# Fewer, longer runs of small products among the large products of a gated DeltaNet decoder layer

## The chip, the cores and the metric

The kernel runs on one core of one Trainium2 chip. The metric is the time of one execution on the device in microseconds (us); lower is better. Three executions of the kernel before took 2884.91, 2886.78 and 2886.98 us, so the median is 2886.78 us.

The core has five engines that run beside one another, each with its own queue. PE multiplies matrices (the profile shows its weight loads apart, as PEld), DVE and ACT do elementwise work and read the products out of PSUM, POOL does some elementwise work in SBUF, and SP issues most of the DMAs. PSUM, into which PE writes, has eight banks; one product of 128 x 512 numbers in fp32 fills a bank.

## What is computed

The reference is one layer of a hybrid decoder with 512 tokens and width 2048. One projection, `h @ w_in`, feeds a branch of sliding-window attention and a branch of gated DeltaNet; the two are merged by gates and projected back. The change touches only the DeltaNet branch:

```python
d_qkv = causal_conv_silu(d_qkv, conv_w)
dq, dk, dv = jnp.split(d_qkv, [DN_KEY, 2 * DN_KEY], axis=-1)
...
t_inv = lax.linalg.triangular_solve(eye + L, ...)
u = t_inv @ v_beta
w = t_inv @ (k_beta * jnp.exp(g)[..., None])
qk = jnp.where(tril, jnp.einsum('bhncd,bhnsd->bhncs', q, k) * decay, 0.0)
...
def step(S, xs):
    u_c, w_c, qk_c, qd_c, kd_c, gl_c = xs
    v_new = u_c - w_c @ S
    o = qd_c @ S + qk_c @ v_new
    S = S * gl_c[..., None, None] + jnp.swapaxes(kd_c, -1, -2) @ v_new
    return S, o
```

There are 16 key heads of width 128 and 32 value heads, two to each key head. The state `S` goes through the sequence; the kernel takes it in four blocks of 128 tokens.

## The kernel before

**Large products.** Every projection is done as large products: weights and activations are split into a high and a low part (ACT casts the high part `whi` on L52, DVE subtracts for `wlo` on L53), and `mm3` (L251) issues three products of 128 x 512 for each block of 128 input channels: L254, L255 and L256. `channel_tile` (L258) makes one tile of 128 output channels by 512 tokens from 16 such blocks, 48 large products into one PSUM bank.

**Small work in steps.** After every second block, thus after every six large products, `channel_tile` calls `pump` (L81). One call of `pump` is called a *step* here. The small work is written as Python generators kept in the list `live`; `yield n` means "go on n steps later" (`step`, L124). So the order of the small work among the large products is fixed when the program is written, in the order of this list within a step. On the chip each engine takes its queue in order and starts each instruction as soon as its inputs are there; work that has its inputs early can run ahead of its step. Beside `live` there are slow generators (`solve`, for the inverse `t_inv` of the second half of the heads, on DVE, in groups 0 to 7) and side generators (`gate`, L1626, from group 8 on: multiply-adds on DVE, L1645, and at its end four products `pgate`, L1653, each of which holds a PSUM buffer until DVE has read it on L1655).

**A head group.** `heads` (L868) runs 16 times, once for a key head and its two value heads. A group makes five channel tiles, q, v0, v1, z0, z1, each with eight steps, so 40 steps; they are numbered 0 to 39 from the group's first. A tile's generator starts on the first step after its tile. What it puts on PE, by the step of its own group (from 40 on, the work lies in the next group's tiles, 40 steps less):

| step | work on PE | function and lines |
|---|---|---|
| 14 | `ptq`: 4 transposes of q | `queries`, L912 and L288 |
| 22 | `ptv` of v0: 4 transposes | `values`, L896 and L288 |
| 23 | `pqk`: query-key product, 8 instructions | `queries`, L951 to L953 |
| 25 | `py`: first product of the joined inverse, 16 instructions of 64 x 64 | L957 to L961 |
| 27 | `pu`: second product of it, 16 instructions of 64 x 64 | L965 to L968 |
| 30 | `ptv` of v1: 4 transposes | `values` |
| 33 | `pv` of block 0 | `scan`, L1000 |
| 35 | `pd` and `po` of block 0 | L1014 to L1021 |
| 37, 39, 41 | block 1: `pp`, `pv`, `pd` and `po` | L992, L1002, L1017 to L1021 |
| 43, 45, 47 | block 2: the same | |
| 49, 51, 53 | block 3: `pp`, `pv`, `po` | |
| 58, 59 | `pto`: 4 transposes of each of the two heads' results | L1056 to L1060 |

An fp32 product of full size is two instructions on PE, a transpose one. Behind `pqk` DVE multiplies it with the masks (tile `E` in the profile, L955); behind `py` DVE copies `Y` (L963); behind `pu` it makes the factors `tt` (L970); between `pp` and `pv` it makes `r` (L995), and between `pv` and `pd` ACT copies `vn` (L1004) and DVE scales `vs` (L1009). After the last block, DVE works out a row scale (L1045 to L1048, some ten short instructions) on step 55 and scales the results `osb` with it on step 56 (L1052). Behind each `pto` DVE multiplies with the gate tile `zh` (L1059); `head_sums` (L1064) sends sums of the two heads to memory from step 70 on. A group's chain thus runs on into the next group's tiles, and small work of two groups is interleaved.

**PSUM.** In this stage the eight banks are: two for the large products (pool `pmm`), two for `ptq`, `ptv`, `pqk`, `py`, `pu`, `pto` and `pgate` (pool `ptp`, tag `tp`), and four for `pp`, `pv`, `po`, `pd` (pool `psc`, tag `sc`). A product waits until the buffer that it is given is free.

After the sixteen groups come two more channel tiles of another kind (`merge_gate`, 16 steps). `drain_live` (L136) then issues what is left of the generators with no large products between, and the next stage, `branch_b`, opens its own PSUM pools over the same banks: six for large products, two for transposes.

Of the kernel before, what the change touches and what calls it, by code (L numbers as in the profile page):

```python
# [7 lines left out]
F32 = mybir.dt.float32  # L8
# [3 lines left out]
ALU = mybir.AluOpType  # L12
# [4 lines left out]
P = 128  # L17
T = 512
D = 2048
KT = D // P  # L20
NTB = T // P
# [4 lines left out]
HD = 64  # L26
# [3 lines left out]
TWO_PI_LO = 3.0199159819567e-07  # L30
MAGIC = float(0x5F3759DF)
NST = 4
NFIRST = 3
STW = 320 + NST * P


class Layer:
# [29 lines left out]

    def go(self, gen, delay=1):

        self.live.append([gen, delay])  # L70

    def paced(self, gen, budget):

# [7 lines left out]
    def pump(self):  # L81
        self.weight_tick()
        with self.behind() if self.keep_order else nullcontext():
            for e in list(self.live):
                e[1] -= 1
                if e[1] <= 0:
                    self.step(e)
        held, self.hold = self.hold > 0, max(self.hold - 1, 0)
        with self.behind():
            for e in [] if held else list(self.slow):  # L90
                e[2] += e[1]
                while e in self.slow and e[2] >= e[3]:
# [22 lines left out]
    def in_turn(self, op):  # L115
# [5 lines left out]
            )  # L121
        self.turn = op.ins.name

    def step(self, e):  # L124
        try:
            e[1] = next(e[0]) or 1
        except StopIteration:
            self.live.remove(e)

# [6 lines left out]
    def drain_live(self):  # L136
        while self.live:
            for e in list(self.live):
                e[1] -= 1
                if e[1] <= 0:  # L140
                    self.step(e)

    def drain_slow(self, e):
# [141 lines left out]
    def transpose4(self, dst, src_cols):  # L285

        for c in range(4):
            self.nc.tensor.transpose(dst[:, c * P : (c + 1) * P], src_cols(c), self.ident)  # L288


    def build(self):
# [599 lines left out]
    def values(self, wk, g, e, ps, st):  # L891
        nc = self.nc
        y = wk.tile([P, T], F32, tag="y", name="yv", bufs=3)
        yield from self.conv(wk, ps, 32 + 2 * g + e, y)
        yield 2
        pt = self.ptp.tile([P, T], F32, tag="tp", name="ptv")  # L896
        self.transpose4(pt, lambda c: y[:, c * P : (c + 1) * P])
        vt = wk.tile([P, NTB, P], F32, tag="vt", name="vt", bufs=3)
        nc.scalar.copy(out=vt.rearrange("p c d -> p (c d)"), in_=pt)
        st[f"v{e}"] = vt  # L900

    def queries(self, wk, g, ps, st):

        nc = self.nc
        sl = lambda c: slice(c * P, (c + 1) * P)
        q = wk.tile([P, T], F32, tag="y", name="yq", bufs=3)
        yield from self.conv(wk, ps, g, q)
        M = [self.decay_load(wk, 2 * g + e) for e in range(2)]
        kT = wk.tile([P, T], F32, tag="kT", name="kT")
        nc.sync.dma_start(out=kT, in_=self.kT_d[g])  # L910
        yield 2
        pt = self.ptp.tile([P, T], F32, tag="tp", name="ptq")  # L912
        self.transpose4(pt, lambda c: q[:, sl(c)])
        ss = self.sumsq(wk, pt)
        yield 3
        epsq = wk.tile([P, NTB], F32, tag="epsq", name="epsq")
        nc.vector.tensor_scalar(out=epsq, in0=ss, scalar1=EPS, scalar2=EPS * P, op0=ALU.add, op1=ALU.mult)
        yield 1
        for e in range(2):
            self.decay_mask(M[e], 2 * g + e)  # L920
        ta = wk.tile([P, NTB, HD], F32, tag="ta", name="ta", bufs=1)
        lab = wk.tile([P, NTB, HD], F32, tag="lab", name="lab", bufs=1)
        ts1 = wk.tile([P, NTB, HD], F32, tag="ts1", name="ts1", bufs=1)
        qd, TT = [], []
        for e in range(2):
            h = 2 * g + e
            qe = wk.tile([P, NTB, P], F32, tag="qe", name="qe", bufs=2)
            nc.sync.dma_start(out=qe.rearrange("p c i -> p (c i)"), in_=self.eg_rows[h].partition_broadcast(P))
            qd.append(qe)
            b, hl = h // 16, h % 16  # L930
            t = self.tt[h % 4]
            for k2 in range(2):
                s = slice(k2 * HD, (k2 + 1) * HD)
                nc.sync.dma_start(out=t[s, :, s], in_=self.ts_d[b, k2, hl].rearrange("c j i -> j c i"))
            s = slice(e * HD, (e + 1) * HD)
            nc.sync.dma_start(out=ta[s], in_=self.ta_d[b, hl].rearrange("c i j -> i c j"))
            nc.sync.dma_start(out=lab[s], in_=self.lab_d[h])
            if e:
# [12 lines left out]
        pqk = self.ptp.tile([P, NTB, P], F32, tag="tp", name="pqk")  # L951
        for c in range(NTB):
            nc.tensor.matmul(pqk[:, c, :], lhsT=kT[:, sl(c)], rhs=q[:, sl(c)], start=True, stop=True)  # L953
        for e in range(2):
            nc.vector.tensor_tensor(out=M[e], in0=pqk, in1=M[e], op=ALU.mult)  # L955
        yield 2
        py = self.ptp.tile([P, NTB, HD], F32, tag="tp", name="py")  # L957
        own = [slice(0, HD), slice(HD, P)]
        for c in range(NTB):
            for e in range(2):  # L960
                nc.tensor.matmul(py[own[1 - e], c, :], lhsT=lab[own[e], c, :], rhs=ta[own[e], c, :], start=True, stop=True)  # L961
        Y = wk.tile([P, NTB, HD], F32, tag="Y", name="Y", bufs=1)
        nc.vector.tensor_copy(out=Y, in_=py)  # L963
        yield 2
        pu = [self.ptp.tile([P, NTB, HD], F32, tag="tp", name="pu") for _ in range(2)]  # L965
        for c in range(NTB):
            nc.tensor.matmul(pu[0][0:HD, c, :], lhsT=Y[HD:P, c, :], rhs=TT[0][HD:P, c, HD:P], start=True, stop=True)
# [12 lines left out]
        yield from self.scan(wk, g, k, kT, TT, qd, M, epsq, st)  # L980

    def scan(self, wk, g, k, kT, TT, qd, M, epsq, st):
        nc = self.nc
        sl = lambda c: slice(c * P, (c + 1) * P)
        v = [st["v0"], st["v1"]]
        osb = wk.tile([P, 2, NTB, P], F32, tag="osb", name="osb", bufs=1)
        osq = wk.tile([P, 2, NTB], F32, tag="osq", name="osq")
        S = None
        for c in range(NTB):
            if c:  # L990
# [3 lines left out]
                for e in range(2):  # L994
                    nc.vector.scalar_tensor_tensor(  # L995
                        out=r[:, e, :], in0=pp[:, e, :], scalar=self.neg_eg[:, c, 2 * g + e : 2 * g + e + 1],
                        in1=v[e][:, c, :], op0=ALU.mult, op1=ALU.add,
# [5 lines left out]
            vn = wk.tile([P, 2, P], F32, tag="vn", name="vn", bufs=2)  # L1003
# [10 lines left out]
            po = self.psc.tile([P, 2, P], F32, tag="sc", name="po")  # L1014
# [3 lines left out]
            for e in range(2):  # L1018
                if c:
                    nc.tensor.matmul(po[:, e, :], lhsT=qd[e][:, c, :], rhs=S[:, e, :], start=True, stop=False)  # L1020
                nc.tensor.matmul(po[:, e, :], lhsT=M[e][:, c, :], rhs=vn[:, e, :], start=c == 0, stop=True)  # L1021
# [28 lines left out]
        for e in range(2):  # L1050
# [1 line left out]
            nc.vector.tensor_tensor(  # L1052
                out=of, in0=of, in1=ro[:, e * NTB : (e + 1) * NTB].unsqueeze(2).to_broadcast([P, NTB, P]), op=ALU.mult
            )
        yield 2
        for e in range(2):  # L1056
            pt = self.ptp.tile([P, T], F32, tag="tp", name="pto")
            self.transpose4(pt, lambda c: osb[:, e, c, :])
            nc.vector.tensor_tensor(out=z[e], in0=pt, in1=z[e], op=ALU.mult)  # L1059
            yield 1  # L1060
        yield 10
        yield from self.head_sums(wk, g, z)

    def head_sums(self, wk, g, z):  # L1064
# [674 lines left out]
```

## Time and profile before

| | us |
|---|---|
| median of three executions | 2886.78 |
| the profiled execution, its own time | 2883.98 |
| span of its records | 2882.2 |
| mean granted PE clock, share of full | 0.997 |
| PE busy | 2831.3 |
| DVE busy | 1869.0 |
| ACT busy | 1138.6 |

The span reaches from the first to the last recorded instruction; 1.8 us of the execution's own time lie outside it. The profile counts an engine as busy while one of its instructions is under way. Products on PE overlap in its pipeline, so the time that a product adds is the distance from its start to the next one's start and not its duration. The DeltaNet groups fill the stretch from about 540 to 1640 us of the span.

### The profile page before, as it was taken

The numbers are of one execution on the slowest core, as the hardware profiler recorded it, in microseconds if no ns is written. First come the engines' busy times: TensorE is split into PE (matmuls) and PEld (weight loads), VectorE is DVE, ScalarE is ACT, GpSimd is POOL, SyncE is SP. The second block draws the span as 40 slices with busy tenths as digits, with TensorE's granted clock in tenths as the row PEclk, the third lists the DMA queues.
The fourth block names the chain that finished last, engine by engine and source line by source line (L and its number), as shares of the span: only waits on it lengthen the run. The fifth ranks groups of instructions, "written<-read, shape, count | busy, mean of one in ns | idle before, by whom it ended". The sixth has DMA issues, their size and how long they took to land.

```text
span 2882.2 us, 38250 instructions
## 1 busy us (share of the span) xinstructions
PE 2831.3 (98%) x14428; PEld 2320.8 (81%) x14428; DVE 1869.0 (65%) x3020; ACT 1138.6 (40%) x2161; POOL 277.2 (10%) x266
## 2 busy tenths in 40 slices
PE   8899999999999999999999999999999999999999
PEld 6677888888888888888877888888887888788787
DVE  6765899777776556666665456665555655554565
ACT  4355333433334333433333355443343434432343
POOL 0013121101111111112110000000100100000000
PEclk9999999999999999999999999999999999999999
DMA  9756555636667867878863377675745647365575
GB/s 379 291 170 198 180 170 157 210 116 208 214 189 206 244 198 245 258 235 243 258 199 103 127 253 263 245 251 195 225 148 163 174 141 223 114 227 185 187 235 164
DMA packets 205471, 590.07 MB, mean 205 GB/s; under 512 B 74564, under 2 KB 99652, under 8 KB 154088
## 3 DMA queue, kind: packets, MB, share of 16 engines
q1 hardware_dynamic: 195080, 529.44, 53.8%
q0 software_dynamic: 10208, 58.20, 10.2%
q8 instruction: 113, 1.85, 0.3%
q14 instruction: 70, 0.57, 0.1%
HBM read 523.79 MB, written 166.40 MB: 239 GB/s over the span
## 4 chain that ended last, share of the span: by engine, by line
PE 85%; DVE 2%; issue 2%; DMA 2%; ACT 1%; POOL 0%; SPq 0%; DVEq 0%; POOLq 0%; ACTq 0%
PE mm L254 20%; PE mm L256 20%; PE mm L255 20%; PE od L254 3%; PE od L255 3%; PE od L256 3%; PE m L255 2%; PE m L256 2%; PE m L254 2%; PE S L1377 1%; PE pv L1002 1%; PE po L1021 1%; PE O L1428 1%; PE pP L288 1%; PE po L1020 1%
## 5 line engine op out<-in xcount | busy, mean ns | idle before, releaser
L254 PE MATMUL mm<-hh,whi 128*128 128x512 f32 x2784 | 1132.6, 407 | 2.3 <-ACT whi L52 1.6
L256 PE MATMUL mm<-hh,wlo 128*128 128x512 f32 x2784 | 1089.6, 391 | 1.0 <-DVE wlo L53 1.0
L255 PE MATMUL mm<-hl,whi 128*128 128x512 f32 x2784 | 1087.4, 391 | 0.0
L53 DVE TENSOR_TENSOR wlo<-raw,whi 128x1024 fp32r<-128x1024 f32 (+1 forms) x476 | 589.1, 1240 | 407.3 <-ACT whi L52 400.1
L52 ACT CAST whi<-raw 128x1024 fp32r<-128x1024 f32 (+1 forms) x476 | 495.3, 1044 | 813.0 <-PE mm L255 692.2
L256 PEld LDWEIGHTS mm<-hh,wlo 128*128 128x128 f32 x2784 | 522.6, 188 | 115.0 <-DVE wlo L53 1.9
L254 PEld LDWEIGHTS mm<-hh,whi 128*128 128x128 f32 x2784 | 523.7, 188 | 113.0 <-issue 9.6
L255 PEld LDWEIGHTS mm<-hl,whi 128*128 128x128 f32 x2784 | 524.2, 188 | 99.3 <-issue 1.4
L255 PE MATMUL od<-wlo,oh 128*128 128x512 f32 x448 | 174.6, 390 | 1.0 <-DVE wlo L53 1.0
L254 PE MATMUL od<-whi,oh 128*128 128x512 f32 x448 | 174.9, 391 | 0.0
L256 PE MATMUL od<-whi,ol 128*128 128x512 f32 x448 | 174.4, 389 | 0.0
L792 POOL TENSOR_TENSOR E<-E,neg_g 128x512 f32<-128x512 f32 x64 | 90.1, 1408 | 492.3 <-DMA E<-g_rows 354.8
L949 POOL TENSOR_TENSOR qe<-qe,yq 128x512 f32<-128x512 f32 x32 | 47.7, 1510 | 853.1 <-DMA qe<-eg_rows 676.4
L844 DVE TENSOR_TENSOR A<-A,atmp 128x62 f32<-128x62 f32 (+30 forms) x124 | 113.4, 914 | 1.5
L837 DVE TENSOR_TENSOR atmp<-A 128x62 f32<-128x62 f32 (+30 forms) x124 | 110.2, 889 | 1.4
L255 PEld LDWEIGHTS od<-wlo,oh 128*128 128x128 f32 x448 | 84.1, 188 | 18.6 <-DVE wlo L53 1.3
L256 PEld LDWEIGHTS od<-whi,ol 128*128 128x128 f32 x448 | 84.1, 188 | 17.6
L254 PEld LDWEIGHTS od<-whi,oh 128*128 128x128 f32 x448 | 84.1, 188 | 17.3 <-ACT whi L52 0.3
L53 DVE TENSOR_TENSOR wlo<-raww,whi 128x1024 fp32r<-128x1024 f32 x56 | 68.4, 1223 | 44.2 <-ACT whi L52 44.2
L52 ACT CAST whi<-raww 128x1024 fp32r<-128x1024 f32 x56 | 58.8, 1054 | 79.3 <-PE m L256 71.8
L995 DVE SCALAR_TENSOR_TENSOR r<-pp,neg_eg,vt 128x128 f32<-128x128 f32 x96 | 29.2, 346 | 73.5 <-PE pp L992 72.3
L1401 ACT ACTIVATE sm<-sm,mx,rs 128x256 f32<-128x256 f32 (+1 forms) x128 | 71.7, 562 | 3.3 <-DVE mx L1396 3.3
(341 smaller groups left out, 3267.1 us busy)
## 6 DMA issues: line engine op xcount, KB each, us to landing
raw<-in_w_ch SPq DMA_DIRECT2D x158, 1024.0 KB
wa<-in_w_ada_ss SPq DMA_DIRECT2D x32, 1024.0 KB
od_m<-in_w_od POOLq DMA_DIRECT2D x32, 1024.0 KB, 13.1
raw<-od_m SPq DMA_DIRECT2D x32, 1024.0 KB
raw<-in_w_od SPq DMA_DIRECT2D x24, 1024.0 KB
E<-g_rows SPq DMA_DIRECT2D x64, 256.0 KB
od_m<-in_w_od SPq DMA_DIRECT2D x16, 1024.0 KB
od_m<-od_m SPq DMA_DIRECT2D x16, 1024.0 KB
```

The costliest lines, as they stand in the source:

```text
L52: self.nc.scalar.copy(out=hi, in_=src)
L53: self.nc.vector.tensor_tensor(out=lo, in0=src, in1=hi.bitcast(F32), op=ALU.subtract)
L254: nc.tensor.matmul(ps, lhsT=wh, rhs=xh, start=first, stop=False)
L255: nc.tensor.matmul(ps, lhsT=wh, rhs=xl, start=False, stop=False)
L256: self.last_mm = nc.tensor.matmul(ps, lhsT=wl, rhs=xh, start=False, stop=last).ins
L288: self.nc.tensor.transpose(dst[:, c * P : (c + 1) * P], src_cols(c), self.ident)
L792: self.in_turn(nc.gpsimd.tensor_tensor(out=E, in0=E, in1=ng, op=ALU.add))
L837: eng.tensor_tensor(out=t, in0=A[:, m : m + 1, m + 1 :].to_broadcast([P, m, n]), in1=A[:, :m, m : m + 1].to_broadcast([P, m, n]), op=ALU.mult,
L844: eng.tensor_tensor(out=A[:, :m, m + 1 :], in0=A[:, :m, m + 1 :], in1=t, op=ALU.add)
L949: self.in_turn(nc.gpsimd.tensor_tensor(out=qf, in0=qf, in1=q, op=ALU.mult))
L995: nc.vector.scalar_tensor_tensor(out=r[:, e, :], in0=pp[:, e, :], scalar=self.neg_eg[:, c, 2 * g + e : 2 * g + e + 1], in1=v[e][:, c, :], ...
L1401: nc.scalar.activation(t, t, AF.Exp, scale=r[:, h : h + 1], bias=mx[:, h : h + 1], accum_out=den[:, h : h + 1])
```

## The change

Four kinds of small work (`ptq`, `ptv` of v0, `pu` and `pto`) are moved so that several come directly behind one another on PE. For this a generator may yield `JOIN + n`: from the next step on it is *late* for up to n + 1 steps, and goes on in the first of these in which another generator has already issued small products (their last instruction's name is left in `self.small`), or in the last of them in any case. Its PE instructions are then made to follow that last small product in PE's order, by an ordering edge without a semaphore (`step_joined`). Late generators are taken after all others of the step, in the list's order.

```diff
     def pump(self):
         self.weight_tick()
         with self.behind() if self.keep_order else nullcontext():
+            self.small = None
+            late = [e for e in self.live if e[2]]
             for e in list(self.live):
-                e[1] -= 1
-                if e[1] <= 0:
-                    self.step(e)
+                if e not in late:
+                    e[1] -= 1
+                    if e[1] <= 0:
+                        self.step(e)
+            for e in late:
+                e[2] -= 1
+                if self.small or not e[2]:
+                    self.step_joined(e)
...
+    def step_joined(self, e):
+
+        n, first = len(self.nc.cur_bb.bb.instructions), self.small
+        self.step(e)
+        for i in self.nc.cur_bb.bb.instructions[n:] if first else []:
+            if i.engine == mybir.EngineType.PE:
+                self.tc.add_manual_dep(
+                    i, first, mybir.DependencyInfo(mybir.DependencyClass.NoSync, mybir.DependencyReason.DATA), reason="join"
+                )
+
     def step(self, e):
+        e[2] = 0
         try:
             e[1] = next(e[0]) or 1
+            if e[1] >= JOIN:
+                e[1], e[2] = 1, e[1] - JOIN + 1
...
@@ values
         yield from self.conv(wk, ps, 32 + 2 * g + e, y)
-        yield 2
+        yield 1
+        yield 1 if e else JOIN + 1
@@ queries, ahead of ptq
-        yield 2
+        yield 1
+        yield JOIN + 1
...
@@ queries, ahead of pu
-        yield 2
-        pu = [self.ptp.tile([P, NTB, HD], F32, tag="tp", name="pu") for _ in range(2)]
+        yield 1
+        yield JOIN + 3
+        pu = [pool.tile([P, NTB, HD], F32, tag=tag, name="pu") for pool, tag in ((self.ptp, "tp"), (self.psc, "sc"))]
...
@@ scan, behind the scaling of osb
-        yield 2
+        yield 3
+        yield JOIN + 2
+        pts = [self.psc.tile([P, T], F32, tag="sc", name="pto") for _ in range(2)]
         for e in range(2):
-            pt = self.ptp.tile([P, T], F32, tag="tp", name="pto")
-            self.transpose4(pt, lambda c: osb[:, e, c, :])
-            nc.vector.tensor_tensor(out=z[e], in0=pt, in1=z[e], op=ALU.mult)
+            self.transpose4(pts[e], lambda c: osb[:, e, c, :])
+        for e in range(2):
+            nc.vector.tensor_tensor(out=z[e], in0=pts[e], in1=z[e], op=ALU.mult)
             yield 1
-        yield 10
+        yield 5
```

`transpose4`, `pqk` and `po` note their last instruction in `self.small`; `drain_live` goes on with late generators at once. The two results' transposes now use the pool `psc`, and so does the second of the two `pu` tiles. No instruction on any engine is added or left out.

More of the change, by code (lines that the diff above doesn't have):

```diff
@@ L32 @@
 NST = 4
+JOIN = 100
 NFIRST = 3
@@ L139, in drain_live @@
                 e[1] -= 1
-                if e[1] <= 0:
+                if e[1] <= 0 or e[2]:
                     self.step(e)
@@ L287, in transpose4 @@
         for c in range(4):
-            self.nc.tensor.transpose(dst[:, c * P : (c + 1) * P], src_cols(c), self.ident)
+            self.small = self.nc.tensor.transpose(dst[:, c * P : (c + 1) * P], src_cols(c), self.ident).ins.name
     def build(self):
@@ L952, in queries @@
         for c in range(NTB):
-            nc.tensor.matmul(pqk[:, c, :], lhsT=kT[:, sl(c)], rhs=q[:, sl(c)], start=True, stop=True)
+            self.small = nc.tensor.matmul(pqk[:, c, :], lhsT=kT[:, sl(c)], rhs=q[:, sl(c)], start=True, stop=True).ins.name
         for e in range(2):
@@ L1020, in scan @@
                     nc.tensor.matmul(po[:, e, :], lhsT=qd[e][:, c, :], rhs=S[:, e, :], start=True, stop=False)
-                nc.tensor.matmul(po[:, e, :], lhsT=M[e][:, c, :], rhs=vn[:, e, :], start=c == 0, stop=True)
+                m = nc.tensor.matmul(po[:, e, :], lhsT=M[e][:, c, :], rhs=vn[:, e, :], start=c == 0, stop=True)
+                self.small = m.ins.name
             nc.scalar.copy(out=osb[:, :, c, :], in_=po)
```

2 lines of the change are left out of this document (1 added, 1 removed).

## The prediction

> **What bounds the kernel now.** I read the page first: shares of the engines and the chain that ended last.
>
> ```profile
> span 2882.2 us, 38250 instructions
> ...
> PE 2831.3 (98%) x14428; PEld 2320.8 (81%) x14428; DVE 1869.0 (65%) x3020; ACT 1138.6 (40%) x2161; POOL 277.2 (10%) x266
> ...
> PE 85%; DVE 2%; issue 2%; DMA 2%; ACT 1%; POOL 0%; SPq 0%; DVEq 0%; POOLq 0%; ACTq 0%
> ```
>
> PE sets the time: it is busy for 98% of the span and 85% of the chain. Then the windows of the DeltaNet groups alone (after the span: PE, PEld, DVE, ACT and POOL busy, the clock, DMA), and the waits of PE from the first group to the next stage.
>
> ```profile
> 560.00:1580.00 1020.00, 1013.88 (x5346) 840.97 (x5345) 688.59 (x1156) 382.30 (x848) 136.35 (x122) 1.00 0.69 208
> ```
> ```profile
> PE pto L288 <- DVE zh L1059: 2.2, 1, 2.2
> PE ptv L288 <- DVE yv L602: 1.6, 3, 0.6
> PE pto L288 <- DVE osb L1052: 1.3, 1, 1.3
> PE pd L1017 <- DVE vs L1009: 0.8, 1, 0.8
> PE pu L967 <- DVE Y L963: 0.7, 1, 0.7
> PE py L961 <- issue: 0.6, 1, 0.6
> PE pv L1002 <- DVE r L995: 0.2, 1, 0.2
> ```
>
> In 1020 us PE idles for 6; all waits of the sixteen groups sum to 7.4 us (2.2 + 1.6 + 1.3 + 0.8 + 0.7 + 0.6 + 0.2). The change leaves every product in place, so it has two sources only: what PE loses when it turns from large products to small ones and back, and these waits. For the first I read PE's timeline around two runs of four transposes.
>
> ```profile
> 684.72 0.39 PE L256 MATMUL mm<-hh,wlo 128*128 128x512 f32 x1
> ...
> 687.44 0.39 PE L256 MATMUL mm<-hh,wlo 128*128 128x512 f32 x1
> 687.67 0.60 PE L288 MATMUL pto<-ident,osb 128*128 128x128 f32 x4
> ...
> 689.50 0.60 PE L288 MATMUL pto<-ident,osb 128*128 128x128 f32 x4
> ...
> 693.82 0.39 PE L256 MATMUL mm<-hh,wlo 128*128 128x512 f32 x1
> ```
>
> From 684.72 to 687.44 twelve large products start undisturbed: 2.72/12 = 0.2267 us each. From 687.44 to 693.82 are 24 of them (1 + 6 + 17) and both runs: 6.38 - 24 x 0.2267 = 0.94 us, so **0.47 us for a run of four**. The attention stage has eight transposes in one run:
>
> ```profile
> 2092.41 0.39 PE L256 MATMUL mm<-hh,wlo 128*128 128x512 f32 x1
> 2092.64 1.03 PE L288 MATMUL pP<-ident,sm 128*128 128x128 f32 x8
> ...
> 2096.03 0.39 PE L256 MATMUL mm<-hh,wlo 128*128 128x512 f32 x1
> ```
>
> Here twelve large products and eight transposes take 3.62 us: 3.62 - 12 x 0.2267 = **0.90 us**. Joining two runs saves 0.94 - 0.90 = 0.04 us. A small product costs its own 0.11 us wherever it stands.
>
> **Where the work goes.** I count steps through the generators. `pu` becomes late on step 26 and finds the v1 transposes on step 30 (27 before). The scan so starts on step 34, not 33, and its last `po` falls on 54, which is step 14 of the next group; there the late `ptq` finds it. With `ptq` on 14 as before, `pqk` stays on 23. The late `pto` (due by 63, so 23; before 58 and 59) and the first `ptv` (due by 23; before 22) both find `pqk`. That leaves 14 runs of the 19 in a group by my count (`po` with `ptq` is one more join than the two in the title). In group 0 there is no earlier scan: `ptq` goes alone on 15, `pqk` on 24, `ptv` on 23. So full-size joins are 15 x 4 (one `ptq`, two `pto`, one `ptv`) = 60, and `pu` makes 16 more.
>
> **Term 1, the joins.** 60 x 0.04 = 2.4 us. Bounds: nothing, and 0.05 each (the start distances are rounded to 0.01), 3.0. For `pu` (products of 64 x 64) no row shows the new neighbour, so I take it from its row alone and the `ptv` behind it:
>
> ```profile
> 567.42 0.39 PE L256 MATMUL mm<-hh,wlo 128*128 128x512 f32 x1
> 567.74 0.27 PE L967 MATMUL pu<-tt,Y 64*64 64x64 f32 x1
> ...
> 572.34 0.39 PE L256 MATMUL mm<-hh,wlo 128*128 128x512 f32 x1
> 572.58 0.60 PE L288 MATMUL ptv<-ident,yv 128*128 128x128 f32 x4
> ```
>
> The first `pu` starts 0.32 us after a large product, the first `ptv` 0.24 after one: entering the smaller shape costs 0.08 more. Behind a transpose it may cost that still, or not. So a join of `pu` saves between 0 and 0.08 + 0.04 = 0.12; I take the middle, 0.06, since nothing is nearer: 16 x 0.06 = 1.0 us (0 to 1.9). Term 1 is **3.4 us (0 to 4.9)**.
>
> The Trainium skill, in "TensorE: Matmul & The Clock Gate", section "Step-by-step: what each phase is for", speaks against it: the drain of one product overlaps the fill of the next, so in a stream each costs its columns alone and the order costs nothing. By that rule term 1 is 0 and only the waits move; the rows above, 0.94 against 0.90, disagree by 0.04 a join.
>
> **Term 2, waits that go.** `pto` waited 2.2 us, once, for its predecessor's buffer while `pgate` held the other of that pool; it now has two of the scan's four, idle on step 23. The first `ptv` waited 0.6 us at most for `yv`; it is now a step (six large products, 1.36 us) and twelve or more small ones later, so its 1.6 goes. `pu` has three steps more for `Y`: 0.7 goes. `py` waited 0.6 when `pqk` and a `pgate` held both buffers:
>
> ```profile
> 1506.06 1.13 PE L1653 MATMUL pgate<-gate_bc,ones 128*128 128x512 f32 x2
> ...
> 1508.41 1.06 PE L953 MATMUL pqk<-yq,kT 128*128 128x128 f32 x8
> ...
> 1511.43 1.28 DVE L955 TENSOR_TENSOR E<-pqk,E 128x512 f32<-128x512 f32 x2
> ...
> 1512.81 0.77 PE L961 MATMUL py<-ta,lab 64*64 64x64 f32 x16 [0.61 <-issue]
> ```
>
> Gone: 2.2 + 1.6 + 0.7 + 0.6 = 5.1 us.
>
> **Term 3, waits that come.** In that same group `ptv`, now behind `pqk`, is the one that needs `pqk`'s buffer, which DVE frees at 1512.7 (1511.43 + 1.28). Eight `pqk` and eight `pto` instructions take some 1.75 us (16 x 0.11), to 1510.2: 2.5 us of wait if nothing stands between, none if large products are put between. All large products queue behind it on PE. I take 1.3. At the end of the groups, the last results wait for their scale (PE's timeline; two pieces of the chain in order of time; DVE's groups in this stage, where 681 is the mean in ns):
>
> ```profile
> 1633.30 0.39 PE L1020 MATMUL po<-S,qe 128*128 128x128 f32 x2
> ```
> ```profile
> 1637.68 0.70 DVE osb L1052
> 1638.43 0.66 PE pto L288 x4
> ```
> ```profile
> L1059 DVE TENSOR_TENSOR zh<-pto,zh 128x512 f32<-128x512 f32 x30 | 20.3, 681 | 0.9 <-PE pto L288 0.8
> ```
>
> From the last `po` to `pto` are 5.13 us, of which 1.3 stall PE. The last `po` comes one step (1.36 us) later while the large products end when they did, so the stall grows to 2.7; and if the next stage's first bank is one of the two that `pto` now holds, it also waits for the multiplication behind the first `pto`, 0.24 longer than the second `pto` covers (0.68 - 0.44). If the next stage's products go first, the 1.3 vanishes. Between -1.3 and +1.6 I take +0.4, near the middle. The waits of `pd` and `pv` (1.0) I leave. Term 3: **+1.7 us (-1.3 to +4.1)**.
>
> **Edits at no cost.** DVE multiplies by the gate tile five steps later; `head_sums` still starts on step 70, so its DMAs keep their place in SP's queue. In groups 1 to 15 `queries` keeps its steps, and with them its loads on SP and its work on POOL. ACT gets `po`'s and `ptq`'s squares on one step instead of two, at 38% busy in this stage (382.30 of 1020). If that cover went, a late `whi` would stall PE once a half tile.
>
> **Sum.** 3.4 + 5.1 - 1.7 = 6.8 us. Against the profiled execution (2883.98: span 2882.2 and 1.8 around it) that is 2877.2; this execution lies 2.8 us under the median 2886.78, so I predict **2880.0 us**, its own range 2876 to 2884.
>
> **Rivals.**
>
> *Waits only move.* DVE is 68% busy here and its queue is in order; a shifted scan meets other splits. Speaking for it: six different products waited, each once or thrice, so no single place makes these waits. Then only term 1 stays: 2886.78 - 3.4 = 2883.4.
>
> *The runs come apart, or joining is worth nothing.* If large products slip between the small ones, so that the change does not do what it says, or if the 0.04 is no more than rounding, terms 2 and 3 alone stay: 5.1 - 1.7 = 3.4 us, 2883.4 again. Against it: 0.94 and 0.90 above, and the eight in one run. (The skill's rule gives this time too.)
>
> *Slower: `r` of block 3.* Its `pp` moves from step 49 to 50, behind all three convolution multiplications of the next q tile in DVE's queue; now it stands between them.
>
> ```profile
> 671.28 0.74 DVE L595 SCALAR_TENSOR_TENSOR yq<-mm,convh,yq 128x511 f32<-128x511 f32 x1
> 671.94 1.15 DVE L837 TENSOR_TENSOR atmp<-A 128x962 f32<-128x962 f32 x1
> 673.01 0.74 DVE L595 SCALAR_TENSOR_TENSOR yq<-mm,convh,yq 128x510 f32<-128x510 f32 x1
> 673.72 0.61 DVE L995 SCALAR_TENSOR_TENSOR r<-pp,neg_eg,vt 128x128 f32<-128x128 f32 x2
> ```
> ```profile
> 673.09 0.59 PE L992 MATMUL pp<-S,kT 128*128 128x256 f32 x2
> ...
> 676.29 0.60 PE L1002 MATMUL pv<-r,tt 128*128 128x128 f32 x4
> ```
>
> From `pp` to its `pv` are 3.20 us; less 0.63 for `pp` and 0.61 for `r`, DVE may be 1.96 us behind before PE stalls. Three multiplications and one of the solver are 3 x 0.74 + 1.15 = 3.4 us, but the first starts at 671.28 and `pp` would come a step later, at 673.09 + 1.36 = 674.45, so about 0.2 is left. Past 1.96 every us costs one in each of 16 groups: at 2.9 behind, 16 x 0.94 = 15 us, less the 6.8: 2895.
>
> *Slower: the clock.* The granted clock, third figure from the end in the windows, fell where a stage had gaps:
>
> ```profile
> 100.00:180.00 80.00, 72.23 (x369) 55.51 (x367) 54.73 (x80) 29.37 (x51) 4.22 (x4) 0.96 0.54 197
> 2060.00:2540.00 480.00, 479.98 (x2755) 384.86 (x2754) 276.13 (x569) 201.31 (x443) 32.93 (x30) 1.00 0.54 166
> ```
>
> A loss of 0.04 x 80 = 3.2 us; once in each of 15 groups, 48 us: about 2928. The second row, attention with its runs of eight transposes, stayed at 1.00. The Trainium skill, same page, section "Part 4: PE-mode transpose", says that transposes don't count as PE activity for the clock, so twelve in a row would be a pause; the attention row does not bear that out for eight.
>
> **How the numbers follow.** Forecast 0.60, moved waits 0.21, runs apart 0.12, late `r` 0.06, clock 0.01. The range **2874 to 2887** takes the bounds of terms 1 and 3 (4.9 + 5.1 + 1.3 = 11.3 at best, so 2875.5, and a few of the remaining waits; 0 + 5.1 - 4.1 = 1.0 at worst, 2885.8) and both rivals at 2883.4, and leaves out the slower two. A change of 0.2%, 5.8 us, is about what a measurement of this kernel tells from none: faster means under 2881.0. The forecast lies just past that, so two thirds of its 0.60 and a quarter of the next two (0.33) count as faster, 0.48; slower 0.07; the same 0.45.
>
> **What would show it.** Right: `pqk`, `pto` and `ptv` follow without a large product between in most groups, `ptq` directly behind `po`, `pu` behind `ptv`; the waits of `pto` for `zh` and of `ptv` for `yv` are gone; a run of twenty costs some 0.12 us less than its four parts. Wrong: `pv` waiting for `r` or `tt` in many groups, a stall of several us ahead of the next stage, a clock under 1.00.

## The result and the profile after

| | us | runs | ratio to before, 95% interval |
|---|---|---|---|
| before | 2886.31 (2883.16 to 2888.83) | 8 | |
| changed | 2894.49 (2892.95 to 2897.53) | 8 | 1.003 (1.0019 to 1.0041) |

The change makes the kernel 8.2 us **slower**. The forecast was 2880.0 us, with a range of 2874 to 2887. The profiled execution of the changed kernel, 2897.53 us, is the slowest of its eight, and that of before, 2883.98, lies below its median; the two traces so differ by 13.5 us where the medians differ by 8.2, and losses read from them add up to 13.5.

Changed kernel, the page: span, busy time, chain by engine.

```profile
span 2895.8 us, 38255 instructions
...
PE 2832.1 (98%) x14428; PEld 2328.1 (80%) x14428; DVE 1875.7 (65%) x3020; ACT 1141.0 (39%) x2161; POOL 281.8 (10%) x266
...
PE 83%; DMA 4%; DVE 3%; issue 2%; ACT 1%; POOL 0%; SPq 0%; DVEq 0%; POOLq 0%; ACTq 0%
```

PE's share of the chain falls from 85 to 83%, and DMA's doubles from 2 to 4%: something on the path now waits for a transfer. Changed kernel, the window of the head groups (columns as in the prediction):

```profile
560.00:1580.00 1020.00, 1003.51 (x5289) 837.81 (x5288) 685.69 (x1137) 379.21 (x843) 139.17 (x122) 0.99 0.69 206
```

PE idles for 16.5 us of these 1020 instead of 6.1, and the granted clock is 0.99 instead of 1.00. Changed kernel, all waits of PE from the first group to the next stage (sum, times, longest):

```profile
PE pd L1041 <- DVE vs L1033: 11.7, 5, 6.1
PE pto L309 <- DVE osb L1077: 3.7, 1, 3.7
PE ptv L309 <- DVE yv L623: 2.7, 4, 1.5
PE ptv L309 <- DVE E L978: 2.1, 1, 2.1
```

The waits of `pto` for `zh`, of `pu`, `py` and `pv` are gone, as forecast. `pd` waits 11.7 us where it waited 0.8, and the last `pto` 3.7 us where it waited 1.3. DVE is named, but DVE isn't the cause. The chain of the changed kernel, in order of time, through the longest of these waits, 6.1 us:

```profile
1445.85 1.21 DVE zh L1086 x2
...
1447.07 19.93 DMA oq_d<-zh
...
1467.11 0.69 ACT zh L905
...
1468.92 0.49 DVE vs L1033 x2
...
1469.46 1.22 PE pd L1041 x2
```

Read it upwards. `pd` waits for `vs`, `vs` for `vn`, which ACT copies; ACT takes its queue in order, and ahead of `vn` stands the copy of the **next** group's gate product into a gate tile `zh`. There are two such tiles. ACT may not write the tile until the store of what the previous group left in it has landed: the store issued at 1447.07 lands at 1467.00, and the copy starts 0.11 us behind that. (The group's other store of a gate tile went at 1450.37 and lands at 1468.49, after the copy has begun, so it is the first that ends this wait.) The same store and copy in the kernel before, its timeline:

```profile
1431.84 1.28 DVE L1059 TENSOR_TENSOR zh<-pto,zh 128x512 f32<-128x512 f32 x2
1433.15 0.37 SPq L1078 DMA_DIRECT2D oq_d<-zh  x1
...
1439.40 0.37 SPq L1078 DMA_DIRECT2D oq_d<-zh  x1
...
1453.94 0.68 ACT L884 ACTIVATE zh<-mm,dnwh 128x512 f32<-128x512 f32 x1
```

No wait stands behind the copy: the stores left 20.8 and 14.5 us ahead of it. Note *when* they left. By the program they belong to step 70 and later, eleven steps (at least 15 us) behind the multiplication by the gate tile. In fact the first was issued as DVE ended it (1431.84 + 1.28 = 1433.12). The stores did not wait for their step, so when the change moved the multiplication five steps on, they went with it: in the changed kernel the first store of every group is issued 0.03 us behind the second multiplication. Call the time from that store's issue to the moment at which ACT is free for the next group's copy into the tile the store's *lead*. Over the groups its median falls from 19.5 us (12.4 to 21.6) in the kernel before to 10.3 us (9.0 to 12.4), and these stores take up to 16.3 and 19.9 us to land. ACT's waits for them, changed kernel and then kernel before, over the groups:

```profile
ACT zh L905 <- DMA oq_d<-zh: 37.2, 9, 10.2
```
```profile
ACT zh L884 <- DMA oq_d<-zh: 3.4, 2, 2.2
```

Why a store takes up to 20 us shows in the DMA view of the changed kernel from 1458 to 1464 us, while ACT waits (queue, packets, MB, share of 16 engines' time):

```profile
q0 software_dynamic: 159, 1.17, 93.8%
q1 hardware_dynamic: 159, 0.16, 9.8%
```

`q0` is POOL's queue, in which the sums of weights (`od_sums`) go from memory to memory, 1.17 MB in 159 packets; `q1` is SP's, with the stores, 1 KB to a packet. The two get as many packets each, and so the stores get a tenth of the engines' time: 159 KB in 6 us, and a store of 256 KB needs about 10 us at that rate (an estimate, 256/159 x 6). From 1464 to 1467 us, with only 34 packets in POOL's queue, the same view has

```profile
q1 hardware_dynamic: 1065, 0.74, 79.3%
```

thus thirteen times as many packets a microsecond ((1065/3) / (159/6) = 13.4). A later store of the same tile, issued at 1523.60 while POOL's queue moves no packet, lands in 2.5 us. The Trainium skill says in "DMA: Bandwidth & Descriptors", section "Queues, rings and completion order", that a DMA engine takes turns between its queues packet by packet; the equal counts, 159 and 159, agree, if a packet of the profile is one of these packets, which no run here shows.

**Where the 13.5 us arise.** Both kernels have the same 10,704 large products, so I compare the start of the n-th one (us after that of the kernel before; product 1000 comes before the first head group, 5760 is the last one ahead of the stall at the end of the groups, 6000 lies in the next stage):

| kernel | 1000 | 3500 | 5760 | 6000 | 10500 |
|---|---|---|---|---|---|
| changed | -2.7 | -4.8 | +7.6 | +12.5 | +13.5 |
| e1, third gate tile | -1.2 | -3.6 | -7.1 | -2.0 | -0.7 |
| e9, end undone | -1.2 | -2.5 | +6.4 | +6.6 | +6.5 |
| e6, both | -2.0 | -4.8 | -8.1 | -7.9 | -8.1 |

(Differences at 1000 are not of the change.) There are **two losses**: in the groups from about the seventh on (3500 to 5760), 12.4 us; and at the end (5760 to 6000), 4.9 us. ACT's first waits for a store, in the third and the fifth group, are of 2.0 and 1.6 us only, and PE does not wait there; from the seventh group on they reach 10.2 us. The second loss is more than its stall. Changed kernel, PE's timeline there, and the window of the first 2 us behind the stall (clock third from the end):

```profile
1644.33 0.40 PE L277 MATMUL mm<-hh,wlo 128*128 128x512 f32 x1
1648.46 1.97 PE L309 MATMUL pto<-ident,osb 128*128 128x128 f32 x8 [3.73 <-DVE osb L1077]
...
1650.65 0.63 PE L276 MATMUL mm<-hl,whi 128*128 128x512 f32 x1
1651.08 0.63 PE L277 MATMUL mm<-hh,wlo 128*128 128x512 f32 x1
...
1653.99 0.40 PE L275 MATMUL mm<-hh,whi 128*128 128x512 f32 x1
1654.22 0.39 PE L276 MATMUL mm<-hl,whi 128*128 128x512 f32 x1
```
```profile
1648.40:1650.40 2.00, 1.94 (x9) 1.94 (x10) 1.30 (x3) 0.00 (x0) 0.00 (x0) 0.50 0.00 0
```

Behind the gap of 3.73 us the clock is 0.50; large products start 0.43 us apart, and from 1653.99 on 0.23. Against the kernel before the stall is 2.4 us longer (3.73 - 1.30), and the slow products cost about as much again. In the kernel before a gap of 1.30 us at this place left the clock at 1.00. The stall itself is longer than reckoned because `wlo` now falls into the middle of the row scale (DVE's timeline, changed kernel):

```profile
1645.87 0.17 DVE L65 SCALAR_TENSOR_TENSOR roy<-rot,roy 128x8 f32<-128x8 f32 x1
1645.98 1.22 DVE L54 TENSOR_TENSOR wlo<-raw,whi 128x1024 fp32r<-128x1024 f32 x1
1647.12 0.16 DVE L63 SCALAR_TENSOR_TENSOR rot<-roy 128x8 f32<-128x8 f32 x1
```

The joins themselves do what they were to do (changed kernel, PE's timeline):

```profile
690.97 0.39 PE L277 MATMUL mm<-hh,wlo 128*128 128x512 f32 x1
691.20 1.05 PE L976 MATMUL pqk<-yq,kT 128*128 128x128 f32 x8
692.09 1.04 PE L309 MATMUL pto<-ident,osb 128*128 128x128 f32 x8
692.96 0.60 PE L309 MATMUL ptv<-ident,yv 128*128 128x128 f32 x4
...
695.95 0.39 PE L277 MATMUL mm<-hh,wlo 128*128 128x512 f32 x1
```

Twenty small products in one run, and twelve large ones: 4.98 - 12 x 0.2267 = 2.26 us. Measured the same way in the kernel before, the four runs cost 0.93, 0.47, 0.48 and 0.47, unrounded 2.34 together (medians over its groups).

### The profile page after: what moved, and what is told of

It is laid out like the page before. It is cut to its first block, busy times and chain, and to the rows that moved or that the text cites. A ratio compares the mean times of both kernels' runs of the same rounds, so it can differ in the third digit from the quotient of the medians.

```text
span 2895.8 us, 38255 instructions
## 1 busy us (share of the span) xinstructions
PE 2832.1 (98%) x14428; PEld 2328.1 (80%) x14428; DVE 1875.7 (65%) x3020; ACT 1141.0 (39%) x2161; POOL 281.8 (10%) x266
## 3 DMA queue, kind: packets, MB, share of 16 engines
q0 software_dynamic: 10208, 58.20, 10.3%
## 4 chain that ended last, share of the span: by engine, by line
PE 83%; DMA 4%; DVE 3%; issue 2%; ACT 1%; POOL 0%; SPq 0%; DVEq 0%; POOLq 0%; ACTq 0%
PE mm L275 19%; PE mm L277 19%; PE mm L276 19%; PE od L276 3%; PE od L275 3%; PE od L277 3%; DMA oq_d<-zh 2%; PE m L276 2%; PE m L277 2%; PE m L275 2%; PE S L1404 1%; PE po L1045 1%; PE O L1455 1%; PE pv L1026 1%; PE pP L309 1%
## 5 line engine op out<-in xcount | busy, mean ns | idle before, releaser
L1047 ACT COPY osb<-po 128x256 f32<-128x256 f32 x64 | 23.9, 373 | 149.7 <-PE po L1045 149.7
```

## The experiments

**The theories.** *S*: the stores of the gate tile, five steps later, land behind the next group's copy; ACT, then `vs`, then `pd` wait. *P*, the rival: the scan lies a step later and the multiplications fall among other work on DVE, so `vs` is late by DVE's queue, and ACT's wait is idle time that costs nothing. Later came *T*, on the end.

**e1: a third gate tile.** To make room, the tiles of the tanh (`th` and `zth`) keep one of their two buffers in this stage (`thb` is 1).

```diff
-tag="z", name="zh", bufs=2)
+tag="z", name="zh", bufs=3)
-th = pool.tile([P, T], F32, tag="th", name="th")
+th = pool.tile([P, T], F32, tag="th", name="th", bufs=self.thb)
```

> The changed kernel with a third buffer for the gate tile zh (and one buffer instead of two for the tanh tile of this stage, to make room). Theory S (store): the gate tile is multiplied five steps later, so it is stored later, and the next group's zh copy on ACT waits for that store with the scan's vn behind it in ACT's queue. Then ACT's wait of zh for the store (37 us in the changed kernel's profile) falls under 5, PE's wait of pd for vs (11.7 us) falls under 2, and the time to 2883 to 2887 against 2894.5 of the changed kernel. Theory P (phase): the waits come from the scan that stands one step later and meets other work on DVE; then pd still waits some 10 us and the time stays at 2892 to 2896.

Measured: 2883.01 us (2880.97 to 2886.24, 11 runs) against 2885.07 (17 runs), ratio 0.9993 (0.9984 to 1.0002). PE's waits:

```profile
PE pto L309 <- DVE osb L1078: 3.7, 1, 3.7
PE ptv L309 <- DVE yv L623: 2.6, 5, 1.1
PE ptv L309 <- DVE E L979: 1.9, 1, 1.9
```

`pd`'s wait is gone, and so is ACT's for the store, with DVE's order as it was; the first stores still leave only 10.2 us (median) ahead of the next group's copy and take up to 19.7 us. The third tile takes away 10 to 11 us of the changed kernel's time (11.5 between the medians, 10.2 with each kernel against the one before that ran beside it). S holds, P falls. But the kernel is only level with before: something else still eats the gain.

**e2: the transposes of the results back in their place, the rest joined.**

```diff
-yield 3
-yield JOIN + 2
-pts = [self.psc.tile(...) for _ in range(2)]
+yield 2
...
-yield 5
+yield 10
```

The two tiles come from `ptp` again, and each is multiplied on its own step.

> The changed kernel with the results' transposes pto put back to two runs, two steps behind the scaling, in the pool ptp; ptq, the first ptv and pu stay joined. Theory S: the store has its lead again, pd's wait for vs falls under 2 us, time 2883 to 2888 (two joins a group, some 1 us, are given up, and pto can wait for a buffer again, 2 us). Theory P: the scan is still a step late, time 2892 to 2896.

Measured: 2908.37 us (2904.09 to 2912.36, 5 runs), ratio 1.0081 (1.0069 to 1.0093). Neither theory has this time. PE's two longest waits:

```profile
PE pto L309 <- DVE osb L1077: 15.6, 8, 4.3
PE pd L1041 <- DVE vs L1033: 7.5, 3, 4.6
```

With the scan still a step later, `pto` two steps behind its scaling comes too early: eight waits for `osb`, with DVE busy. So the later `pto` is not a free choice once the scan is later; it covers the scaling. `pd` did not fall under 2 us either, as theory S had it: ACT still waits 15.9 us for the store, five times, and the lead is 14.2 us in the median, between the 10.3 of the changed kernel and the 19.5 of the one before. The experiment undid one thing and brought another, and does not separate the theories.

**e3: `pu` and `ptq` back in their place, the transposes of results and values still joined to `pqk`.** The scan then lies where it lay before the change.

```diff
-yield 1
-yield JOIN + 3
+yield 2
...
-yield 1
-yield JOIN + 1
+yield 2
...
-yield JOIN + 2
+yield JOIN + 3
```

The pieces stand ahead of `pu`, of `ptq` and of `pto`.

> The changed kernel with pu and ptq put back to their old steps, so that the scan starts on step 33 as before; pto and the first ptv stay joined to the query-key product on step 23. Theory S: the store is as late as in the changed kernel, pd or another product of the scan still waits some 10 us in all, time 2892 to 2898. Theory P: the waits go, time 2882 to 2887.

Measured: 2897.29 us (2891.27 to 2900.51, 6 runs), ratio 1.0038 (1.0025 to 1.0051). Of PE's and of ACT's waits:

```profile
PE pd L1039 <- DVE vs L1031: 18.1, 5, 7.6
```
```profile
ACT zh L905 <- DMA oq_d<-zh: 35.4, 8, 10.3
```

The scan's own place is not the cause: with it as before the loss is all there. (The last `pto` waits 1.3 us, as before, so this loss lies in the groups.)

**e4: the kernel before, with only the result transposes five steps later.** No joins.

```diff
-yield 2
+yield 7
-pt = self.ptp.tile([P, T], F32, tag="tp", name="pto")
+pt = self.psc.tile([P, T], F32, tag="sc", name="pto")
-yield 10
+yield 5
```

> The kernel before with one thing moved: pto's two runs stand five steps later (and in the pool psc), with no join anywhere. Theory S: the late gate multiplication alone makes the loss, so ACT waits over 20 us for the store, PE over 8 us for vs, and the time is 2893 to 2898. Theory P: the scan stands where it stood, time 2884 to 2888.

Measured: 2895.55 us (2890.47 to 2897.71, 5 runs), ratio 1.0033 (1.0021 to 1.0045).

```profile
PE pd L1017 <- DVE vs L1009: 9.0, 6, 4.2
```
```profile
ACT zh L884 <- DMA oq_d<-zh: 26.9, 8, 6.9
```

This edit alone costs 10.5 us and brings both waits, with a lead of 11.6 us in the median. It is enough to make the loss, which needs no join.

**e5: control, the kernel before with the third gate tile** (e1's edit).

> The kernel before with the third zh buffer and the single tanh buffer, nothing else: the control of e1_three_z. Theory S (store late by five steps): the old kernel's zh waited only 3.4 us for the store and PE 0.8 for vs, so it gains at most 1 us: 2884 to 2886. A rival, that a third zh buffer is a gain by itself whatever the order of the products: some 10 us less, as in e1_three_z against the changed kernel, 2873 to 2877.

Measured: 2884.82 us (2880.58 to 2893.51, 11 runs) against 2885.87 (22 runs), ratio 0.9996 (0.9987 to 1.0005). ACT's waits for the store are gone here too. The third tile is worth nothing measurable by itself; what it gives in e1 is the loss that the change brought.

**e6: e1, and the last group not held back.**

```diff
-yield JOIN + 3
+yield JOIN + 3 if g < KH - 1 else 1
...
-yield 3
-yield JOIN + 2
+yield 3 if g < KH - 1 else 1
+yield JOIN + 2 if g < KH - 1 else 1
```

> e1_three_z, and in the last group pu, the scan and pto stand as before the change. If the scan's later end makes the 3.7 us for which the last pto waits for the scaled results, that wait returns to about 1.3 and the time falls by 2 us, to about 2881; if the wait comes from the banks of the pool psc alone, it stays at 3 to 4.

Measured: **2876.62 us** (2875.09 to 2878.82, 7 runs), ratio 0.997 (0.9958 to 0.9982): faster than both kernels, by 9.3 us than the one before.

```profile
PE ptv L309 <- DVE yv L623: 2.4, 4, 1.1
...
PE pto L309 <- DVE osb L1078: 1.3, 1, 1.3
```

The stall at the end falls by 2.4 us, as it should, but the time by 6.4 and not by 2 (by 7.2 with each against the kernel before that ran beside it). The table of large products has most of the missing part at the end, between products 5760 and 6000: e1 loses 5.0 us there to the kernel before (from -7.07 to -2.03), e6 0.2. That led to theory **T**: the price of a long stall is the stall and, behind it, products at half the clock.

**e7: e6, with the first values' transposes in a buffer of the scan's pool**, so that they need not wait for `pqk`'s.

```diff
-pt = self.ptp.tile([P, T], F32, tag="tp", name="ptv")
+pool, tag = (self.ptp, "tp") if e else (self.psc, "sc")
+pt = pool.tile([P, T], F32, tag=tag, name="ptv")
```

> e6_three_z_end, with the first values' transposes in the pool psc, so that they never wait for the buffer that the query-key product or a pgate holds: ptv's wait for E (1.9 us in e1_three_z) goes and the time falls by another 2 us, to 2878 to 2880. If the buffer is not the cause, ptv still waits.

Measured: 2878.82 us (2876.6 to 2880.75, 10 runs), ratio 0.9975 (0.9966 to 0.9984): not faster than e6. The wait for `E` goes, but others come: a large product waits 1.0 us for DVE's `zh`, `py` 0.4 us, and `ptv` for `yv` has 3.0 us instead of 2.4. A miss: the time lies in the expected range by luck, since that range was set 2 us under an e6 of 2881 that came out at 2876.62.

**e8: the changed kernel with all sums of weights issued at the end of the stage**, so that POOL's queue is empty in the groups.

```diff
-self.beside(self.ordered(self.od_sums()), 0.13, "ws")
+self.beside(self.ordered(self.od_sums()), 0.0, "ws")
```

> The changed kernel, with the sums of output weights (copies and additions of 1 MB from memory to memory, issued beside groups 2 to 15) all issued at the end of the groups instead. The total rises by some 100 us and more, since the next stage waits for them; what counts is the groups' stretch. If the store of zh lands late because these transfers share the DMA engines with its packets of 1 KB, ACT's wait of zh for the store falls from 37 us to under 5 and PE's wait of pd for vs to under 1. If the five steps alone make it late, both stay at about 37 and 12.

Measured, one execution: 3131.76 us, as the next stage then waits 228 us for the sums; only the groups are of use. In them ACT has no wait for the store left, and `pd` none for `vs`, with two gate tiles and the short lead (median 10.2 us): the first store of each group now lands in 2.1 to 3.4 us. From product 1000 to 5760 e8 loses 0.5 us to the kernel before, where the changed one loses 10.3. The DMA view of e8, 1440 to 1470 us:

```profile
q1 hardware_dynamic: 2752, 5.70, 56.3%
```

POOL's queue has no row, and the engines are 56% busy. So it takes both: the lead that the change took from the stores, and DMA engines that another queue fills.

**e9: the changed kernel with only the end undone** (e6's edit, two gate tiles).

> The changed kernel, in which only the last head group is not held back (its second inverse product, scan and result transposes keep the steps of before); the gate tile keeps two buffers. Theory S with the end (T): the changed kernel loses twice, by the stores of the gate tile inside the groups and, apart from that, at the end, where the result transposes stall 3.73 us for the scaled results instead of 1.30 and the products behind the stall run at a granted clock of 0.50 for some 5 us (start distances 0.43 instead of 0.23 us). By the traces the end costs 5.3 us, of them 2.4 stall and the rest clock: 2894.5 - 5.2 = 2889.3 (2888 to 2891), with ACT's wait of the gate tile's copy for its store (37 us) and PE's of the state update for the scaled values (about 12 us) as they were. Rival: the end is worth the longer stall alone, 2.4 us: 2892.1; the rest of what the kernel with three buffers gained by the same edit was something else.

Measured: 2891.2 us (2887.9 to 2894.33, 9 runs) against 2885.04 (25 runs), ratio 1.002 (1.001 to 1.003). The median lies between the two theories' times, nearer the rival's 2892.1, and its runs spread over 6 us; it doesn't decide. The trace speaks for the larger price: from product 5760 to 6000 e9 loses 0.2 us to the kernel before, where the changed one loses 4.9. PE's waits are as expected; ACT's for the store is not, 26.1 us in seven waits instead of 37:

```profile
PE pd L1041 <- DVE vs L1033: 10.8, 5, 6.5
...
PE pto L309 <- DVE osb L1077: 1.3, 1, 1.3
```

**e10: e1 with ten more large products in the last stall.** They stand behind the last `merge_gate`, and nothing reads them.

```diff
+ft = self.ptp.tile([P, T], F32, tag="tp", name="fill")
+for c in range(10):
+    nc.tensor.matmul(ft, lhsT=self.hh[:, c, 0:P], rhs=self.hl[:, c, :], start=c == 0, stop=c == 9)
 self.drain_live()
```

> The changed kernel with three gate buffers, and ten more large products of 128 x 512 (of the layer's input with itself, into a buffer that nothing reads) behind the last large product of the groups, where PE then stalls 3.73 us for the scaled results. The output is unchanged. They take 10 x 0.23 = 2.3 us of the stall, so that 1.4 us of it is left. Theory T: the half clock behind the stall comes of the length of the gap on PE; a gap of 1.3 us in the kernel before left the clock at 1.00, one of 3.73 brought 0.50. Then no product behind it runs slow, and work added makes the kernel faster by 2.4 us (the rest of the end's 5.3 behind the stall's 2.4, less some tenths): 2883.0 - 2.4 = 2880.6. Rival: the products behind a wait for the last results run slow whatever PE does in it: 2883.0, unchanged. The Trainium skill, in 'TensorE: Matmul & The Clock Gate', section 'HAM oscillation - how this bites in real kernels', has the rule that PE's clock halves behind a gap of over 3.4 us; theory T is that rule at this place.

Measured: 2880.2 us (2877.11 to 2882.55, 11 runs), ratio 0.9983 (0.9974 to 0.9992); e1 had 2883.01 beside a kernel before at 2885.07. More work, 2.8 us less time by the medians; the two intervals overlap, so the traces have to bear it out. PE's timeline of e10, and the window behind the stall:

```profile
1630.44 2.45 PE L698 MATMUL fill<-hl,hh 128*128 128x512 f32 x10
1634.33 1.32 PE L309 MATMUL pto<-ident,osb 128*128 128x128 f32 x8 [1.44 <-DVE osb L1081]
1635.41 0.48 PE L275 MATMUL mm<-hh,whi 128*128 128x512 f32 x1
1635.72 0.39 PE L276 MATMUL mm<-hl,whi 128*128 128x512 f32 x1
```
```profile
1634.20:1638.20 4.00, 3.83 (x20) 3.17 (x21) 3.56 (x8) 0.00 (x0) 0.00 (x0) 1.00 0.19 66
```

The same eight `pto` take 1.32 us instead of 1.97, and large products start 0.23 apart at once. From the large product ahead of the stall to the twentieth behind it, less 0.2267 for each of the twenty, e10 takes 5.08 us, its ten added products among them, and e1 7.50. At this place it is the gap's length that lowers the clock, and T holds.

**e11: the same with twenty transposes.**

```diff
+for c in range(20):
+    nc.tensor.transpose(ft[:, (c % 4) * P : (c % 4 + 1) * P], self.ident, self.ident)
```

> As the kernel with ten large products in the last stall, but the filling is twenty transposes of 128 x 128 (of the identity, into a buffer that nothing reads), 20 x 0.11 = 2.2 us. The output is unchanged. If any instruction keeps the clock: no product behind the stall runs slow, 2880.6, as with large products. If transposes do not keep it: the clock falls to 0.50 behind the stall as without filling, 2883.0. The Trainium skill's page 'TensorE: Matmul & The Clock Gate', section 'Part 4: PE-mode transpose', says that transposes do not count as activity for the clock, which is the second case.

Measured: 2879.38 us (2876.82 to 2882.34, 11 runs), ratio 0.9979 (0.997 to 0.9987). The window behind the stall:

```profile
1633.40:1637.40 4.00, 3.91 (x21) 3.21 (x22) 3.48 (x7) 0.00 (x0) 0.00 (x0) 1.00 0.19 66
```

Transposes hold the clock here as large products do.

## Why the prediction was wrong, step by step

**The bound and the counting were right.** PE bounds the kernel, and the steps come out as counted: 14.4 runs a group for 19.2 before, `po` with `ptq`, `pqk` with `pto` and `ptv`, `ptv` with `pu`.

**Term 1 was right in kind and somewhat large.** By medians over the groups, `po` with `ptq` costs 1.346 us for 0.921 + 0.471, the run of twenty 2.252 for 2.342, `ptv` with `pu` 1.279 for 0.492 + 0.839: 0.046 + 0.090 + 0.052 = 0.188 us a group, 2.8 us in fifteen, for a forecast of 3.4. (These costs count the eleven large products behind each run; over four the same sum gives 1.8 us, so its size is known to about 1 us.) The four full-size joins give 0.034 each (forecast 0.04), `pu` 0.05 (0.06). The Trainium skill says ("TensorE: Matmul & The Clock Gate", "Step-by-step: what each phase is for") that the drain of one product overlaps the fill of the next; the prediction took from this, as the other possibility, that the order costs nothing. By the count above a join saves 0.03 to 0.05 us.

**Term 2 was right in part.** Of its four waits, three went, 3.5 of the 5.1 us. `ptv`'s for `yv` did not: 1.6 us in three became 2.7 in four. Of these, 1.05 us in two are the moved first `ptv`, whose `yv` is late in some groups even a step on, and 1.65 in two the second values' `ptv`, which did not move.

**Term 3 failed at the end.** `ptv` behind `pqk` waits 2.1 us, within its bounds of 0 and 2.5. The last `pto` was set at +0.4, with 1.6 as the upper end, and it costs 4.9 (changed kernel, products 5760 to 6000). Three things went into that. The middle of the range was taken though the likely order, small work ahead of the next stage, gave +1.4 by itself. The step that shifted the last `po` also put `wlo` into the row scale, so the stall is 3.73 and not 2.7. And a stall was priced at its own length, while the half clock behind it costs another 2.4 us (7.50 less 5.08 us, see e10). The rival *clock* had a price near the measured one (3.2 us for a place, against 2.4) and the wrong place: runs of twenty small products leave the clock at 1.00, stalls do not.

**The step that failed above all is "Edits at no cost".** It said: "DVE multiplies by the gate tile five steps later; `head_sums` still starts on step 70, so its DMAs keep their place in SP's queue". A step fixes the order of an engine's queue and not the time. SP had nothing ahead of the stores that held them, so they left when DVE was done, and five steps later with it. Their lead fell from 19.5 us to 10.3, and this the prediction put at nothing. By e1 it costs 10 to 11 us, by e4 10.5. It also undoes the statement that the change "has two sources only", the turns of PE and the waits already there: the loss is a new wait. The kernel before held the evidence in one row of ACT's waits, which the prediction does not show, where the copy into `zh` already waits 3.4 us for the stores in two groups: in these the lead was just used up. What is asked of any moved step is who reuses the tile that it frees.

**The sum without the two losses was near, in part by luck.** From product 1000 to 5760 e1 gains 5.9 us on the kernel before and e6 6.2. The forecast for that stretch, without the end, was 3.4 + 5.1 - 1.3 = 7.2 us. Of e6's 6.2 us the joins are 2.8 and shorter waits of PE 1.9 (7.4 against 5.5), where 3.8 was forecast; 1.5 us are not placed.

**The other rivals.** `pv` never waits for `r`, so the late `r` of block 3 did not come. The runs did not come apart. That the waits only move (2883.4) is closest in kind, though what came was a new wait, by a transfer, and not an old one elsewhere.

**What stays open**: what makes a store take 5.5 us in one group and 19.9 in another while the sums run, and the 1.5 us of the gain. The price of the end is read from traces; the medians of the changed kernel and e9 differ by 3.3 us, those of e1 and e6 by 6.4.

## What to carry to other kernels

When a step is moved later, list the tiles that it and what follows it release, and look who writes them next and how much lead is left, engine by engine in the trace's times and not in the program's steps; a copy that waits for a store holds everything behind it in its engine's queue. Price a PE stall of over some 2 us at more than its length (at the end of this stage a stall of 3.73 us cost 2.4 us more). A delay that pays in a loop is to be left out in the last turn, where nothing covers it.

## What the runs showed that was not expected

**The clock falls behind shorter gaps than thought.** These are all gaps on PE of over 1.1 us from 150 us on, in the profiled executions of all thirteen kernels, with the clock granted in the 1.5 us behind. Up to 1.96 us it was 0.87 or more. Of nine gaps from 2.09 to 2.26 us four brought it to between 0.50 and 0.77; of nineteen from 2.51 us on eighteen brought it to between 0.50 and 0.71, and one of 3.38 us left it at 1.00. This is one of the shorter ones, in the changed kernel, PE's timeline:

```profile
992.39 0.39 PE L277 MATMUL mm<-hh,wlo 128*128 128x512 f32 x1
995.60 1.22 PE L1041 MATMUL pd<-vs,k 128*128 128x256 f32 x2 [2.82 <-DVE vs L1033]
996.62 0.64 PE L1044 MATMUL po<-S,qe 128*128 128x128 f32 x2
```

The `po` behind it take 0.64 us and not 0.39, so part of the loss in the groups is slow products, as at the end. The Trainium skill's rule in "TensorE: Matmul & The Clock Gate", "HAM oscillation — how this bites in real kernels", is that gaps of over some 3.4 us bring half the clock; that agrees for the long ones, but here 2.5 us were enough in nearly all cases. Its section "Part 4: PE-mode transpose", that transposes don't count as activity, is not borne out by e11: 2.2 us of them in a gap kept the clock at 1.00.

**A store of 256 KB took up to 19.9 us to land** beside another queue with packets seven times as large (1.17 MB against 0.16 in as many packets). With that queue empty the same store took 2.1 to 3.4 us as the first of its group (e8). What it takes is here set by the packets that it shares the engines with, more than by its own size.
